# Starting a feed-forward network's activations 0 to 48 bytes into their buffers

## The chip, the cores and the metric

The kernel runs on one core of one Trainium2 chip. The time is the device time of one execution in microseconds (us); lower is better. TensorE multiplies matrices, ScalarE (ACT) and VectorE (DVE) do the element-wise work, and the on-chip memory that they share is SBUF: 128 partitions, each a long row of bytes. An operand of an instruction is a stretch of bytes at the same place in every partition. This document is about where in the partition such a stretch begins.

## The reference

The reference is a two-layer encoder over 256 tokens of width 2048, all in float32. Each layer has an attention half and a feed-forward half. Cut to what matters here, the feed-forward half is:

```
h = rmsnorm(x, norm_ffn[l]) * (1.0 + sc_m) + sh_m          # (256, 2048)
g, v = split(h @ w_up[l])                                  # 2 x (256, 5632)
u = silu(conv3(g)) * conv3(v)                              # depthwise over the tokens
x = x + gt_m * (u @ w_down[l])                             # back to (256, 2048)
```

The product `u` is what the kernel calls an activation; w_down is applied to it.

## The kernel before

**Layout.** Features lie on the 128 partitions and tokens along the partition, so the 5632 hidden features are 44 chunks of 128. A float32 number is kept as a sum of two numbers of a shorter type (fp32r): a high part and what is left over, the low part. An activation of one chunk is therefore `[P, 2, S]`: 256 high values and then 256 low ones, 2,048 bytes in a row of each partition. `split` (L349) writes them, the high half with an ACT instruction (L350) and the low half with a DVE one (L351).

**Products.** `feature_run` (L230) multiplies. For each block of weights and each activation there is a *wide* matmul, whose moving operand is all 512 columns of the activation (high and low) against the weights' high part (L248 or L253), and a *narrow* one, whose moving operand is the 256 high columns against the weights' low part (L250). The two together are called a *pair* below. With `joint` set there are three narrow ones instead (L239, L240, L241). The moving operand is the one that streams through TensorE; the stationary one is a 128x128 block of weights in `hl` and is loaded by an LDWEIGHTS (PEld in the profile) ahead of its matmul.

**Order.** The weights are read in units of 1 MB through four buffers, split into high and low parts by ACT (L225) and DVE (L226) into four `hl` buffers, and used in the order in which they arrive. The feed-forward half goes through the 44 chunks in three groups of 15, 16 and 13 (`FF_GROUPS`, L37; the loop at L830). For each group the up-projections fill the activations of the group, and then the down-projection (`down`, L869) runs over the 16 output blocks, each of which needs every chunk of the group. So each activation is the moving operand of 16 pairs; in the last group the last output block is joint, which makes 15 pairs and three narrow matmuls for each chunk. The tile planner orders each engine's instructions by their dependencies; the stretches that this document speaks of have no other order written by hand.

**Buffers.** `place` (L147) gives out the stage buffers. There are seven, known by a tag, and every use of a tag gets the same bytes: y0, y1, y2 (4 x 1,024 bytes in each partition), a, b0, b1 (12 x 1,024) and o (16 x 1,024). In the compiled program they lie one behind the other in that order, from byte 163,296 of the partition to byte 228,832:

| buffer | first byte | modulo 64 | modulo 512 | held by turns |
|---|---|---|---|---|
| y0, y1, y2 | 163296, 167392, 171488 | 32 | 480 | outputs of attention A, gate B, activations |
| a | 175584 | 32 | 480 | q, k, v of A; outputs of attention B; activations |
| b0, b1 | 187872, 200160 | 32 | 480 | q, k, v of B; outputs of attention B (b0); activations |
| o | 212448 | 32 | 480 | gate A; activations |

Everything else that TensorE reads as fp32r has its own place: the four `hl` buffers begin at byte 70,688, and the buffer that holds the normed input `h` or the merged branches `merged` begins at 103,456. These are all 32 modulo 64 and 32 modulo 512. Blocks within a buffer are multiples of 512 bytes apart, so these remainders hold for every fp32r operand. The padded rows `cpad` of the convolution are an exception of another kind: they are 1,032 bytes long, and ACT and DVE read and write them 0, 4 and 8 bytes from their start (L347, L824, L826).

The activations of the groups go into these buffers (two rows of 1,024 bytes for each chunk): groups 0 and 2 use o for eight chunks and a for the next (six in group 0, five in group 2), and group 0 puts its last chunk in y0; group 1 uses b0 and b1 for six each and y1 and y2 for two each.

Of the kernel before, what the change touches and what calls it, by code (L numbers as in the profile page):

```python
# [10 lines left out]
F32R = mybir.dt.float32r  # L11
# [4 lines left out]
P = 128  # L16
L = 2
D = 2048
S = 256
# [41 lines left out]

ATT = [1.288, 0.4]
ATT_B = [0.21, 0.21]

ADA_ORDER = [[p * KC + k for k in range(KC) for p in ps] for ps in ((0, 1), (2,), (3, 4), (5,))]
ADA_ORDER = [i for part in ADA_ORDER for i in part]
# [38 lines left out]
def encoder(ctx: ExitStack, tc: tile.TileContext, a: dict, out: bass.AP):  # L105
# [20 lines left out]
    for i in range(3):  # L126
        t = const.tile([P, S + 2], F32, name=f"cpad{i}")
# [16 lines left out]
    x = const.tile([P, KC, S], F32, name="x")  # L144
    sp = pool("s", 1)

    def place(tag, n, dt, name):  # L147
        return sp.tile([P, n, S], dt, name=name, tag=tag)

    mods, amods, nrms, done = {}, {}, {}, {0: 0, 1: 0}  # L150

# [197 lines left out]
    def split(dst, src):  # L349
        nc.scalar.copy(dst[:, 0], src)  # L350
        nc.vector.tensor_tensor(out=dst[:, 1], in0=src, in1=dst[:, 0].bitcast(F32), op=ALU.subtract)  # L351
# [169 lines left out]
    def urgent(yes):  # L521
        return tc.high_priority() if yes else nullcontext()
# [21 lines left out]
    def need(l, n):  # L544

        while done[l] < n:
            next(adas)
# [15 lines left out]

    mean_sq = sm.tile([P, 2], F32, name="ms_in", tag="nsa")
    acc = place("y0", 4, F32, "sq_in")
    for i in range(0, KC, 4):
        sq = acc if i == 0 else place(f"y{1 + i // 4 % 2}", 4, F32, f"sq_in{i}")
        nc.scalar.activation(out=sq[:], in_=x[:, i : i + 4], func=AF.Square)
        if i:
            nc.vector.tensor_tensor(out=acc[:], in0=acc[:], in1=sq[:], op=ALU.add)  # L570
# [31 lines left out]
    for l in range(L):  # L602
# [14 lines left out]


        packs = [place("a", 12, F32, f"packA{l}"), place("b0", 12, F32, f"packB{l}_0"), place("b1", 12, F32, f"packB{l}_1")]
        kTa, qTa = packs[0][:, 0:3:2], packs[0][:, 4:12]  # L620

# [125 lines left out]
        for mo in range(KC):  # L747
# [4 lines left out]
            st.features(oA, [proj_a], joint=joint)  # L752
        bg.pace(job, ATT_B[l])
        gb = []
        for tag in ("y0", "y1", "y2"):
            t = place(tag, 4, F32, f"gb{l}_{tag}")
            gb += [t[:, i] for i in range(4)]
        for i in range(2):
            t = ev.tile([P, 2, S], F32, name=f"gb{l}_{i}", tag="u", bufs=2)
# [22 lines left out]
        def residual(ps, mo, part, joint):  # L782

            gt = mod[:, part * KC + mo : part * KC + mo + 1]
            for half in ([slice(0, S)] if joint else [slice(S, 2 * S), slice(0, S)]):
                nc.vector.scalar_tensor_tensor(  # L786
                    out=x[:, mo], in0=ps[:, half], scalar=gt, in1=x[:, mo], op0=ALU.mult, op1=ALU.add
                )
# [30 lines left out]
        def conv(ps, ch, u):  # L819
            pad = cpad[ncp[0] % 3]  # L820
            ncp[0] += 1
            sum_halves(ps, pad[:, 1 : S + 1])
            w = cw[:, ch]
            nc.scalar.activation(out=u, in_=pad[:, 1 : S + 1], func=AF.Identity, scale=w[:, 1:2], bias=w[:, 3:4])  # L824
            for j, o in ((0, 0), (2, 2)):
                nc.vector.scalar_tensor_tensor(  # L826
                    out=u, in0=pad[:, o : o + S], scalar=w[:, j : j + 1], in1=u, op0=ALU.mult, op1=ALU.add
                )

        for gi, chunks in enumerate(FF_GROUPS):  # L830
            acts = []
            for tag, n in (("b0", 12), ("b1", 12), ("y1", 4), ("y2", 4)) if gi % 2 else (("o", 16), ("a", 12), ("y0", 4)):
                if len(acts) < len(chunks):
                    t = place(tag, n, F32R, f"act{l}_{gi}_{tag}")
                    acts += [t[:, i : i + 2] for i in range(0, n, 2)]
            acts = dict(zip(chunks, acts))
            sil = {}

            def g_evac(ps, c):
                u = sil[c] = ev.tile([P, 2, S], F32, name="u", tag="u", bufs=2)  # L840
                conv(ps, c, u[:, 0])
                nc.scalar.activation(out=u[:, 0], in_=u[:, 0], func=AF.Silu)

            def v_evac(ps, c):
                u = sil.pop(c)
                conv(ps, FC + c, u[:, 1])
                nc.vector.tensor_tensor(out=u[:, 1], in0=u[:, 1], in1=u[:, 0], op=ALU.mult)
                split(acts[c], u[:, 1])

            todo = list(chunks)  # L850
            if gi == 0:
                c0, c1 = todo[:2]
                todo = todo[2:]
                st.features(
                    hs, [lambda p: g_evac(p, c0), lambda p: v_evac(p, c0), lambda p: g_evac(p, c1), lambda p: v_evac(p, c1)]
                )
            for c in todo:
                st.features(hs, [lambda p: g_evac(p, c)])
                st.features(hs, [lambda p: v_evac(p, c)])
            if gi == len(FF_GROUPS) - 1:  # L860
                sums = Squares(f"ssf{l}") if l < L - 1 else None
            else:
                sums = None
            if gi == 0:
                need(l, 96)

            last = gi == len(FF_GROUPS) - 1

            def down(mo):  # L869
                def evac(ps):  # L870
                    residual(ps, mo, 5, last and mo >= ENDING)
                    if last:
                        if l < L - 1:
                            sums.add(mo)
                        else:
                            nc.sync.dma_start(out[:, mo], x[:, mo])

                return evac

            for mos in OUT_TURNS:  # L880
                end = mos[0] == KC - 1
                ending = last and mos[0] >= ENDING
                if last and end and l < L - 1:
                    nxt = Stream(l + 1)
                    nxt.prefetch(AHEAD)
                with urgent(ending):
                    st.features(
                        [acts[c] for c in chunks], [down(mo) for mo in mos], sums.first if sums and end else None, joint=ending
                    )
# [75 lines left out]
```

## Time and profile before

| | |
|---|---|
| median of 3 runs | 2775.12 us (2775.0 to 2776.88) |
| the profiled execution: its time | 2775.14 us |
| the profiled execution: its span, first to last instruction | 2773.4 us |
| mean granted TensorE clock | 0.991 |
| PE busy | 2715.0 us, 98% of the span |
| DVE busy, ACT busy | 2214.0 us (80%), 1450.3 us (52%) |

The profile is of one execution. An entry "L250 PE MATMUL ps<-act_o,hl" is a matmul issued at line 250, written to a tile named ps, with moving operand act_o (an activation in buffer o) and weights in hl. A matmul's own duration is longer than its turn, since the next one enters while it drains; the turn is the distance from one start to the next, and is read from views that merge a run of equal matmuls into one piece, or from a stretch's length over its matmuls. The chain of waits follows the work that ended last back from the end of the program.

### The profile page before, as it was taken

The page shows a single profiled execution, that of the slowest core. Times are in us where ns is not written, and L with a number is a line of the kernel's source. Part 1 is how long each engine was busy: PE and PEld are TensorE (multiplying, and loading weights), DVE is VectorE, ACT ScalarE, POOL GpSimd, SP SyncE. Part 2 cuts the span into 40 slices and gives each one's busy share as a digit, 9 for nine tenths or more (in the row PEclk, how much of TensorE's full clock was granted, in tenths as well). Part 3 has the DMA queues.
Part 4 walks back from the last instruction along what each step waited for, and adds up shares of the span by engine and source line. Part 5 has one row for each costly group of instructions (what it writes and reads, how often), then busy time and mean ns, then how long its engine had stood idle before and what let it go on. Part 6 is the DMA issues. An engine that isn't in the chain of part 4 may idle for free.

```text
span 2773.4 us, 39861 instructions
## 1 busy us (share of the span) xinstructions
PE 2715.0 (98%) x15930; PEld 2398.7 (86%) x15930; DVE 2214.0 (80%) x3163; ACT 1450.3 (52%) x2137; POOL 39.3 (1%) x24
## 2 busy tenths in 40 slices
PE   7899999999999999999999999999989999999999
PEld 5788799998888888888878888888878888888888
DVE  6998987897999888789976666768989767766775
ACT  5344684444654455355544567555455535544553
POOL 0000100000000000000000000000000000000000
PEclk9999999999999999999999999999999999999999
DMA  8887588896778766777756666665867655555553
GB/s 314 334 329 264 214 308 329 329 331 231 279 279 328 276 255 245 271 274 286 291 190 238 228 227 233 232 254 199 306 222 287 243 190 187 193 186 194 184 196 137
DMA packets 101852, 699.72 MB, mean 252 GB/s; under 512 B 12705, under 2 KB 15009, under 8 KB 17697
## 3 DMA queue, kind: packets, MB, share of 16 engines
q1 hardware_dynamic: 101666, 697.17, 68.2%
q8 instruction: 125, 2.05, 0.3%
q14 instruction: 61, 0.50, 0.1%
HBM read 695.03 MB, written 2.10 MB: 251 GB/s over the span
## 4 chain that ended last, share of the span: by engine, by line
PE 79%; issue 14%; DVE 4%; POOL 1%; ACT 1%; DMA 0%; POOLq 0%; SPq 0%; ACTq 0%; DVEq 0%
PE ps L253 20%; PE ps L250 18%; PE ps L248 15%; PE ps_t L338 4%; PE ps L240 4%; PE ps L239 4%; PE ps L241 4%; PE ps_t L339 4%; PE ps_t L337 4%; DVE aw L162 1%; DVE hl L226 1%; POOL qrs L390 1%; PE sc L485 1%; PE po L516 1%; ACT hl L225 0%
## 5 line engine op out<-in xcount | busy, mean ns | idle before, releaser
L226 DVE TENSOR_TENSOR hl<-w,hl 128x1024 fp32r<-128x1024 f32 x928 | 1131.3, 1223 | 307.6 <-ACT hl L225 300.8
L225 ACT CAST hl<-w 128x1024 fp32r<-128x1024 f32 x928 | 972.5, 1050 | 756.3 <-PE ps L253 174.5
L162 DVE CUSTOM_DVE_ANT_0 aw<-aw,cact,ab 128x2048 f32<-128x2048 f32 x192 | 450.7, 2347 | 25.5 <-DMA aw<-in_aw 25.1
L250 PEld LDWEIGHTS ps<-h,hl 128*128 128x128 f32 x3328 | 428.0, 191 | 16.9
L250 PE MATMUL ps<-h,hl 128*128 128x256 f32 x3328 | 432.9, 283 | 0.0
L253 PE MATMUL ps<-h,hl 128*128 128x512 f32 x1712 | 428.7, 392 | 0.0
L248 PE MATMUL ps<-h,hl 128*128 128x512 f32 x1616 | 406.4, 394 | 5.5 <-DVE cpad L347 4.5
L248 PEld LDWEIGHTS ps<-h,hl 128*128 128x128 f32 x1616 | 306.3, 190 | 70.8 <-DVE cpad L347 5.4
L253 PEld LDWEIGHTS ps<-h,hl 128*128 128x128 f32 x1712 | 307.9, 189 | 55.0
L346 ACT COPY r<-ps 128x256 f32<-128x256 f32 x240 | 88.9, 372 | 286.0 <-PE ps L253 286.0
L337 PE MATMUL ps_t<-hl,h 128*128 128x512 f32 x576 | 228.1, 401 | 7.5 <-ACT hl L225 7.0
L338 PE MATMUL ps_t<-hl,h 128*128 128x512 f32 x576 | 228.6, 397 | 4.7 <-DVE hl L226 4.7
L339 PE MATMUL ps_t<-hl,h 128*128 128x512 f32 x576 | 227.6, 396 | 0.9 <-DVE h L426 0.9
L826 DVE SCALAR_TENSOR_TENSOR u<-cpad,cw,u 128x256 f32<-128x256 f32 x352 | 168.7, 481 | 7.6 <-ACT u L824 3.2
L241 PE MATMUL ps<-h,hl 128*128 128x256 f32 x512 | 145.9, 285 | 0.0
L239 PE MATMUL ps<-h,hl 128*128 128x256 f32 x512 | 145.3, 284 | 0.0
L240 PE MATMUL ps<-h,hl 128*128 128x256 f32 x512 | 145.0, 283 | 0.0
L786 DVE SCALAR_TENSOR_TENSOR x<-ps,mod,x 128x256 f32<-128x256 f32 x237 | 111.5, 481 | 40.5 <-PE ps L253 30.4
L337 PEld LDWEIGHTS ps_t<-hl,h 128*128 128x128 f32 x576 | 109.8, 191 | 31.1 <-ACT hl L225 7.6
L338 PEld LDWEIGHTS ps_t<-hl,h 128*128 128x128 f32 x576 | 110.0, 191 | 30.8 <-DVE hl L226 8.1
L339 PEld LDWEIGHTS ps_t<-hl,h 128*128 128x128 f32 x576 | 109.9, 191 | 24.3 <-DVE h L426 1.4
L347 DVE TENSOR_TENSOR cpad<-ps,r 128x256 f32<-128x256 f32 x176 | 74.4, 424 | 63.2 <-ACT r L346 63.0
(202 smaller groups left out, 3610.4 us busy)
## 6 DMA issues: line engine op xcount, KB each, us to landing
w<-in_ws SPq DMA_DIRECT2D x464, 1024.0 KB, 4.9
aw<-in_aw SPq DMA_DIRECT2D x192, 1024.0 KB, 4.9
bias<-in_bias SPq DMA_DIRECT2D x16, 256.0 KB, 4.4
x<-in_xT SPq DMA_DIRECT2D x4, 512.0 KB, 5.6
out<-x SPq DMA_DIRECT2D x16, 128.0 KB, 1.8
cw<-in_cw SPq DMA_DIRECT2D x2, 176.0 KB, 4.0
maskA<-in_maskA SPq DMA_DIRECT2D x1, 256.0 KB, 5.3
ab<-in_ab SPq DMA_DIRECT2D x2, 48.0 KB, 7.1
```

What stands on the lines that cost most here:

```text
L162: nc.vector.tensor_tensor_reduce(out=raw[:], in0=raw[:], in1=cact[:], scale=1.0, scalar=ab[:, i : i + 1], op0=ALU.mult, op1=ALU.add, accum ...
L225: nc.scalar.copy(hl[:, 0], r)
L226: nc.vector.tensor_tensor(out=hl[:, 1], in0=r, in1=hl[:, 0].bitcast(F32), op=ALU.subtract)
L239: nc.tensor.matmul(out[:, 0], hi, act[:, 0], start=first, stop=False)
L240: nc.tensor.matmul(out[:, 0], hi, act[:, 1], start=False, stop=False)
L241: nc.tensor.matmul(out[:, 0], lo, act[:, 0], start=False, stop=last)
L248: nc.tensor.matmul(o, w, act, start=first, stop=False)
L250: nc.tensor.matmul(o, w, act, start=False, stop=False)
L253: nc.tensor.matmul(o, w, act, start=False, stop=last)
L337: nc.tensor.matmul(ps[:], xh, hi, start=kc == kcs[0], stop=False)
L338: nc.tensor.matmul(ps[:], xh, lo, start=False, stop=False)
L339: nc.tensor.matmul(ps[:], xl, hi, start=False, stop=kc == kcs[-1])
```

## The change

`place` makes each stage buffer 16 elements (64 bytes) longer and takes an optional `skip` in bytes, by which the view that it returns is moved into the buffer. Seven buffers 64 bytes longer lie one behind the other, so each also moves by 64 bytes for each buffer ahead of it, whatever it holds. The activations alone ask for a skip, from a table by layer and group:

```
+ACT_SKIP = [
+    [{"o": 16, "a": 16}, {"b0": 16, "b1": 32}, {"o": 32, "a": 32}],
+    [{"o": 48, "a": 48}, {"b0": 32, "b1": 48}, {"o": 0, "a": 0}],
+]
...
-    def place(tag, n, dt, name):
-        return sp.tile([P, n, S], dt, name=name, tag=tag)
+    def place(tag, n, dt, name, skip=0):
+
+        t = sp.tile([P, n * S + 16], dt, name=name, tag=tag)
+        return t[:, skip // 4 : skip // 4 + n * S].rearrange("p (n s) -> p n s", s=S)
...
-                    t = place(tag, n, F32R, f"act{l}_{gi}_{tag}")
+                    t = place(tag, n, F32R, f"act{l}_{gi}_{tag}", ACT_SKIP[l][gi].get(tag, 0))
```

No instruction is added or removed, and none has another shape. Tags that are not in the table (y0, y1, y2) get no skip. What is computed stays the same.

## The prediction

> **What bounds the kernel now.** I read the page first, then the stages in which the activations are used, then the pace of single matmuls.
>
> ```profile
> span 2773.4 us, 39861 instructions
> PE 2715.0 (98%) x15930; PEld 2398.7 (86%) x15930; DVE 2214.0 (80%) x3163; ACT 1450.3 (52%) x2137; POOL 39.3 (1%) x24
> ...
> PE 79%; issue 14%; DVE 4%; POOL 1%; ACT 1%; DMA 0%; POOLq 0%; SPq 0%; ACTq 0%; DVEq 0%
> ```
>
> TensorE is busy for 98% of the span and carries the chain of waits. What an operand's place can change is therefore first of all the turn of a matmul. The activations are read in the six down-projections (layer 0 groups 0, 1, 2, then layer 1). One row for each, from the view of stretches:
>
> ```profile
> core 0: us, PE busy (x) PEld busy (x) DVE busy (x) ACT busy (x) POOL busy (x), PEclk, DMA share, GB/s
> 843.50:926.90 83.40, 83.40 (x482) 72.63 (x482) 72.91 (x92) 32.69 (x33) 0.00 (x0) 1.00 0.83 319
> 1104.90:1193.80 88.90, 88.90 (x514) 77.40 (x513) 69.58 (x84) 34.87 (x35) 0.00 (x0) 1.00 0.70 262
> 1338.40:1411.00 72.60, 72.60 (x432) 63.53 (x430) 58.98 (x82) 33.47 (x44) 0.00 (x0) 1.00 0.70 256
> 2202.20:2285.60 83.40, 83.40 (x482) 72.66 (x481) 51.41 (x65) 32.75 (x33) 0.00 (x0) 1.00 0.54 190
> 2463.60:2552.50 88.90, 88.90 (x514) 77.40 (x513) 55.21 (x67) 34.86 (x35) 0.00 (x0) 1.00 0.54 192
> 2697.10:2769.40 72.30, 72.30 (x430) 63.27 (x428) 42.62 (x57) 25.38 (x26) 0.00 (x0) 1.00 0.43 152
> sum 489.50, PE 489.50 PEld 426.89 DVE 350.71 ACT 194.02 POOL 0.00; mean PE 81.58 PEld 71.15 DVE 58.45 ACT 32.34 POOL 0.00
> ```
>
> In all six, PE busy equals the length of the stretch at a granted clock of 1.00: nothing is waited for, and every nanosecond that a matmul gains or loses here moves the end by as much. The whole lever is 489.5 us. DVE is the next engine (72.91 of 83.40 us), so TensorE could be 10 us faster in that stage before DVE's splitting of weights limits it.
>
> Now the pace. The chain, first in an up-projection (moving operand h), then in the first down-projection (activations); columns are start, length, what:
>
> ```profile
> 806.55 1.91 PE ps L250 x16
> 808.47 1.84 PE ps L253 x8
> 810.31 1.81 PE ps L248 x8
> ...
> ```
> ```profile
> 845.57 1.83 PE ps L250 x16
> 847.40 1.86 PE ps L253 x8
> 849.26 0.91 PE ps L250 x8
> 850.17 1.86 PE ps L253 x8
> ```
>
> A narrow matmul takes 1.91/16 = 119.4 ns with h and 0.91/8 = 113.75 ns with an activation. A wide one takes 230 then 226.3 ns with h (1.84/8, 1.81/8; mean 228.1) and 232.5 ns with an activation (1.86/8). The sums are nearly equal: 347.5 ns for a pair with h, 346.25 ns with an activation. The same difference shows where all matmuls are narrow, layer 0's projection of the outputs of attention B (oB, 384 matmuls) and the output projection behind it (merged, 768 matmuls):
>
> ```profile
> 524.50:568.04 43.54, 43.54 (x386) 1.00 0.78 288
> 568.04:660.44 92.40, 92.40 (x772) 1.00 0.89 327
> ```
>
> 43.54/384 = 113.4 ns and 92.40/768 = 120.3 ns. Clock, form and code are the same; oB begins at 480 modulo 512 and merged at 32, like the weights. So the place of a moving operand relative to the weights seems to have a price, some 6.9 ns a matmul, and the wide ones pay it where the narrow ones don't. All fp32r operands of this trace begin 32 past a multiple of 64: what 16, 48 or 0 past such a multiple costs, no row shows.
>
> **The change part by part.** With 64 bytes more for each buffer the starts without skip become, modulo 512: y0 480, y1 32, y2 96, a 160, b0 224, b1 288, o 352; all are still 32 modulo 64. The skips are added to that, so it is a skip of 32 that reaches a multiple of 64, and not a skip of 0. Counted in pairs (16 for a chunk; 15 in the last groups, with three narrow ones beside):
>
> - 16 or 48 past a multiple of 64 (skips 16 and 48): 14 + 14 chunks of both groups 0, b0 of layer 0 and b1 of layer 1, 40 chunks, 640 pairs.
> - a multiple of 64 (skip 32): 13 chunks of layer 0's group 2 (195 pairs, 39 narrow), b1 of layer 0, b0 of layer 1 (192): 387 pairs.
> - still 32 past: 10 chunks in y0, y1, y2 and the 13 of layer 1's group 2: 355 pairs. With the others that is 1382; all but y0's 32 change place relative to the weights, 1350.
>
> *Writing.* ACT and DVE write the activations, 88 instructions each. Whether their place has a price is shown by cpad, which is written and read 4 bytes off, against aligned tiles:
>
> ```profile
> L347 DVE TENSOR_TENSOR cpad<-ps,r x176: 414/426/428, 696.6 to 2697.7; 128x256 f32<-128x256 f32 x176
> L347 DVE TENSOR_TENSOR z<-ps,r x48: 418/425/426, 1750.9 to 1930.2; 128x256 f32<-128x256 f32 x48
> ```
> ```profile
> L350 ACT CAST act_o<-u x32: 388/407/408, 702.2 to 2645.6; 128x256 fp32r<-128x256 f32 x32
> L351 DVE TENSOR_TENSOR act_o<-u,act_o x32: 417/418/423, 704.2 to 2646.6; 128x256 fp32r<-128x256 f32 x32
> ```
>
> 426 against 425 ns: nothing. I take 0. The cover would be the up-projections, in which the chain runs on TensorE; if writing took twice as long and that cover were gone it would be 88 x (407 + 418) = 73 us, and a gain is bounded by the same cover at 0.
>
> *Place relative to the weights, activations.* Bounds for a pair from the chain's rows: best 113.75 + 226.3 = 340.0 ns, worst 119.4 + 232.5 = 351.9, so -6.2 to +5.7 ns against 346.25, and for 1350 pairs -8.4 to +7.7 us. At both places that the trace shows the price falls on one of the two and the sum hardly differs, so I take the nearest known sum for each: the 64 pairs of y1 (at 32, as h) +1.25 ns, 0.1 us; 0 for the others.
>
> *The same for the attention's outputs, layer 0, three narrow matmuls for each head and output block.* oB: 384 matmuls, a at 160 and b0 at 224, between the known 480 (113.4) and 32 (120.3). Bounds 0 (no run of narrow ones is faster) and 384 x 6.9 = 2.6 us; neither end is nearer, I take half, 1.3 us. Attention A's outputs in y1 and y2 (two heads each, 96 matmuls each): y1 at 32 pays it all, 0.7 us; y2 half, 0.3 us. In layer 1 these are pairs: 0.
>
> *The start itself, 640 pairs at 16 or 48, 387 at 0.* Nothing in the trace prices it. Nearest rows: cpad (0) on the low side, and the 6.9 ns step on the high side, as what one more access might cost: 640 x 2 x 6.9 = +8.8 us for the first, and the same step as a gain, 387 x 2 x 6.9 + 39 x 6.9 = -5.6 us, for the second. I take 0 for both, by cpad, the only row where a start is off, though on another engine. [...]
>
> *The longer buffers* shift addresses and nothing else; no DMA, wait or instruction is added, and none is moved in a queue (SP's and POOL's included).
>
> Sum: 0.1 + 1.3 + 0.7 + 0.3 = +2.4 us on 2775.14 us of the profiled execution (span 2773.4 and 1.7 around it; the median of the runs, 2775.12, is the same): **2777.5 us**. A change under 0.2% (5.6 us) is about what a measurement of this kernel can't tell from none, so my forecast is "no change".
>
> **The rivals.**
>
> *Slower, one more access (2786 us).* If a start 16 past a multiple of 32 costs each read one more access of 6.9 ns: +8.8 us. For it speaks that TensorE's turn does depend on low address bits (113.4 against 120.3); against it, that the step seen belongs to the relation with the weights. Past 5.6 us with the +2.4 it decides from (5.6 - 2.4)/1280 = 2.5 ns a matmul.
>
> *Much slower, halved reading.* If TensorE fetches in aligned 32-byte words and a start of 16 splits each of them, 640 pairs take up to twice their turn: 640 x 346.25 = +222 us, 2999 us. Nothing in the trace speaks for it but that it never happens there: all starts are 32 past.
>
> *Faster (2769 us).* If the present start of 32 past a multiple of 64 already costs an access in every matmul, the 387 pairs gain 5.6 us, and another 387 x 6.2 = 2.4 us if their wide ones go at 226.3 ns: -8.0 us, 2769.5. For it: no start on a multiple of 64 has been seen, so the pace of now may not be TensorE's own. Against: narrow and wide differ by 226.3 - 113.75 = 112.5 ns for 256 columns, so most of a turn is proportional to the columns and no fixed extra shows. [...]
>
> **How the numbers follow.** No price of the start, place within ±5.6 us: 0.45, 2777.5 us. One more access: 0.24. Halved, wholly or in part: 0.12. Faster: 0.19. So faster 0.19, same 0.45, slower 0.24 + 0.12 = 0.36. The range leaves out the halved reading (0.12) and little else: up to 2777.5 + 8.8 + 7.7 + 1.3, about 2795 (one more access and the worst place together), down to 2769.5 with some 3.5 us of the gain by place, 2766.
>
> **What would show it.** The six stretches of the down-projections keep their lengths: 83.4, 88.9 and 72.6 us in layer 0. Layer 0's group 0 against layer 1's group 0 tells 16 from 48; group 2 of layer 0 against that of layer 1 tells 0 from 32 modulo 64. oB's 113.4 ns rise toward 120. One more access shows as both groups 0 longer by 14 x 16 x 13.8 ns = 3.1 us; halved reading as over 100 us there. L350 and L351 stay at 407 and 418 ns. The prediction is wrong if a moving operand's pace depends on 16 or 64 bytes, or if the planner, given buffers of another shape, orders the instructions differently.

## The result: 0.28% slower

The changed kernel takes 2781.68 us (median of 12 runs, 2779.99 to 2787.64) against 2774.22 us (12 runs, 2772.51 to 2776.88): ratio 1.0028, 95% interval 1.0019 to 1.0037. The profiled execution took 2779.99 us.

The page of the changed kernel:

```profile
span 2778.2 us, 39861 instructions
...
PE 2717.4 (98%) x15930; PEld 2402.4 (86%) x15930; DVE 2215.0 (80%) x3163; ACT 1449.4 (52%) x2137; POOL 39.3 (1%) x24
```

The same instructions, in the same order on every engine, and TensorE is still the bound. The stretches that matter, in the changed kernel: first layer 0's projection of oB, then the six down-projections (start and end, length, busy time of each engine, granted clock):

```profile
core 0: us, PE busy (x) PEld busy (x) DVE busy (x) ACT busy (x) POOL busy (x), PEclk, DMA share, GB/s
523.49:569.14 45.65, 45.65 (x387) 45.65 (x385) 43.92 (x72) 21.56 (x31) 0.00 (x0) 1.00 0.77 287
843.25:927.63 84.38, 84.38 (x482) 73.70 (x481) 73.04 (x92) 32.63 (x33) 0.00 (x0) 1.00 0.84 316
1105.62:1195.76 90.14, 90.14 (x514) 78.65 (x513) 69.72 (x84) 34.79 (x35) 0.00 (x0) 1.00 0.69 258
1340.37:1414.13 73.76, 73.76 (x432) 64.52 (x430) 58.95 (x82) 33.56 (x44) 0.00 (x0) 1.00 0.68 253
2204.83:2289.01 84.18, 84.18 (x482) 73.46 (x481) 51.36 (x65) 32.70 (x33) 0.00 (x0) 1.00 0.52 189
2467.00:2557.03 90.03, 90.03 (x514) 78.49 (x513) 55.20 (x67) 34.82 (x35) 0.00 (x0) 1.00 0.54 189
2701.63:2774.28 72.65, 72.65 (x430) 63.81 (x428) 42.60 (x57) 25.32 (x26) 0.00 (x0) 1.00 0.44 152
```

The down-projections sum to 495.1 us, 5.6 us more than before (489.5), each still wholly busy at a granted clock of 1.00. oB's projection takes 45.65 us instead of 43.54, 2.1 us more. Together 7.7 us, about the 7.5 us by which the medians differ. (The two profiled executions differ by only 4.9 us. The one of the changed kernel starts oB 1.0 us earlier, it is 1.4 us shorter between oB and the first down-projection, and 0.5 us shorter between the down-projections of layer 0 and those of layer 1. The opening part differs from kernel to kernel: oB starts at 522.6 to 525.7 us in the runs below that leave `h` where it was.)

The pace, from the changed kernel's chain in the first down-projection (start, length, what):

```profile
845.26 1.90 PE ps L257 x16
847.16 1.85 PE ps L260 x8
849.01 0.95 PE ps L257 x8
849.96 1.85 PE ps L260 x8
```

A narrow matmul (L257, formerly L250) now takes 0.95/8 = 118.75 ns instead of 113.75, a wide one 1.85/8 = 231 instead of 232.5. Further on the same chain has pieces of 0.93 and 1.87 us (116 and 234 ns); the pair takes 350 ns in either case, 3.75 ns more than before. Over the whole stretch, from each start to the next, the narrow ones go from 114.0 to 118.5 ns on average and the wide ones from 232.8 to 232.4, so the loss lies in the narrow ones. It isn't confined to what moved: buffer y0 is first in the pool and has no skip, so the chunk in it begins where it did. In the first down-projection its narrow matmuls last 277 ns each before and 282 after, with 113.9 and 118.1 ns from each start to the next (the groups of that stretch; behind the bar busy us, then mean ns), first before, then after:

```profile
L250 PE MATMUL ps<-act_y,hl 128*128 128x256 f32 x16 | 4.1, 277 | 0.0
```
```profile
L257 PE MATMUL ps<-act_y,hl 128*128 128x256 f32 x16 | 4.2, 282 | 0.0
```

### The profile page after: what moved, and what is told of

Read it like the earlier page. It is cut to its first block, busy times and chain, and to the rows that moved or that the text cites. A ratio compares the mean times of both kernels' runs of the same rounds, so it can differ in the third digit from the quotient of the medians.

```text
span 2778.2 us, 39861 instructions
## 1 busy us (share of the span) xinstructions
PE 2717.4 (98%) x15930; PEld 2402.4 (86%) x15930; DVE 2215.0 (80%) x3163; ACT 1449.4 (52%) x2137; POOL 39.3 (1%) x24
## 4 chain that ended last, share of the span: by engine, by line
PE 79%; issue 14%; DVE 4%; POOL 1%; ACT 1%; DMA 1%; POOLq 0%; SPq 0%; ACTq 0%; DVEq 0%
PE ps L260 19%; PE ps L257 18%; PE ps L255 15%; PE ps_t L345 4%; PE ps_t L346 4%; PE ps L246 4%; PE ps L247 4%; PE ps L248 4%; PE ps_t L344 4%; DVE aw L169 1%; DVE hl L233 1%; POOL qrs L397 1%; PE sc L492 1%; PE po L523 1%; DMA aw<-in_aw 0%
## 5 line engine op out<-in xcount | busy, mean ns | idle before, releaser
L257 PEld LDWEIGHTS ps<-h,hl 128*128 128x128 f32 x3328 | 427.7, 191 | 16.9
L257 PE MATMUL ps<-h,hl 128*128 128x256 f32 x3328 | 432.7, 283 | 0.0
```

What stands on the lines that cost most here:

```text
L257: nc.tensor.matmul(o, w, act, start=False, stop=False)
```

## The experiments

Two theories to begin with. S: the start of an operand modulo 32 or 64 has a price. P: its place relative to the weights has one. *Distance* below is the start of the moving operand less that of the weights.

**The longer buffers alone.**

```
 ACT_SKIP = [
-    [{"o": 16, "a": 16}, {"b0": 16, "b1": 32}, {"o": 32, "a": 32}],
-    [{"o": 48, "a": 48}, {"b0": 32, "b1": 48}, {"o": 0, "a": 0}],
+    [{"o": 0, "a": 0}, {"b0": 0, "b1": 0}, {"o": 0, "a": 0}],
+    [{"o": 0, "a": 0}, {"b0": 0, "b1": 0}, {"o": 0, "a": 0}],
```

> The changed kernel with every skip set to 0: the buffers stay 64 bytes longer, so each moves by 64 bytes for each buffer ahead of it, and every start is again 32 past a multiple of 64. Theory P (what counts is where a moving operand lies relative to the weights in some stretch of up to 512 bytes): the loss stays; the six down-projections are together 4 to 7 us longer than before (489.5 us), the projection of oB in layer 0 takes about 45.6 us as in the changed kernel instead of 43.5, and the whole is about 0.25% slower than before. Theory S (what counts is the start modulo 32 or 64): the down-projections return to 83.4, 88.9, 72.6, 83.4, 88.9, 72.3 us and the whole is within 0.1% of before.

Ratio 1.0015 (1.0005 to 1.0025). The same stretches in this kernel:

```profile
522.57:568.21 45.64, 45.64 (x386) 45.64 (x385) 43.91 (x72) 21.58 (x31) 0.00 (x0) 1.00 0.79 287
843.84:927.67 83.83, 83.83 (x482) 73.47 (x481) 72.86 (x92) 32.57 (x33) 0.00 (x0) 1.00 0.85 319
1105.65:1195.10 89.45, 89.45 (x514) 78.17 (x513) 69.68 (x84) 34.85 (x35) 0.00 (x0) 1.00 0.71 261
1339.67:1412.51 72.84, 72.84 (x432) 64.02 (x430) 58.88 (x82) 33.53 (x44) 0.00 (x0) 1.00 0.68 256
2203.84:2287.67 83.83, 83.83 (x482) 73.47 (x481) 51.41 (x65) 32.65 (x33) 0.00 (x0) 1.00 0.53 190
2465.65:2555.09 89.44, 89.44 (x514) 78.16 (x513) 55.21 (x67) 34.80 (x35) 0.00 (x0) 1.00 0.53 190
2699.66:2772.31 72.65, 72.65 (x430) 63.82 (x428) 42.61 (x57) 25.32 (x26) 0.00 (x0) 1.00 0.44 151
```

Without any skip, oB's loss is there in full (45.64) and the down-projections sum to 492.0 us, +2.5. So the skips add the other 3.1 us, and layer 1's group 2, whose skip was 0, has the same 72.65 us in both. The down-projections lost less than the 4 to 7 us expected by P, and the whole 0.15% instead of 0.25%. Still, 4.6 of the 7.7 us come from the longer buffers alone, with which every start stays 32 past a multiple of 64: S alone can't be it.

**The skip alone, in buffer o.** o is last in the pool, so only its own length changes.

```
-        t = sp.tile([P, n * S + 16], dt, name=name, tag=tag)
+        t = sp.tile([P, n * S + (16 if tag == "o" else 0)], dt, name=name, tag=tag)
...
+    [{"o": 16}, {}, {"o": 32}],
+    [{"o": 48}, {}, {"o": 0}],
```

> Only buffer o, the last one, is longer, and only the activations in it are skipped: 16, 32, 48 and 0 bytes in layer 0 groups 0 and 2 and layer 1 groups 0 and 2. Every other operand stays where it was before. o holds 8 of 15 or 13 chunks. Theory S: layer 0 group 0 and layer 1 group 0 become longer by the share of o, about 0.5 us each (8/15 of the 0.8 to 1.0 us lost in the changed kernel), and layer 0 group 2 by about 0.7 us. Theory P in its strict form (only whole steps of 64 bytes count): layer 0 group 0 at 48 stays at 83.4 us, and the other two change as far as they pass into the next 64 bytes. The second groups and layer 1 group 2 stay at 88.9 and 72.3 us by both.

Ratio 1.0013 (1.0004 to 1.0022). The three groups with a skip:

```profile
843.30:927.82 84.52, 84.52 (x482) 73.64 (x481) 73.07 (x92) 32.64 (x33) 0.00 (x0) 1.00 0.84 315
...
1339.32:1412.72 73.40, 73.40 (x432) 64.35 (x430) 58.88 (x82) 33.54 (x44) 0.00 (x0) 1.00 0.71 254
2202.55:2287.00 84.45, 84.45 (x482) 73.61 (x481) 51.44 (x65) 32.71 (x33) 0.00 (x0) 1.00 0.53 188
```

+1.1, +0.8 and +1.05 us; the other three groups kept their lengths to 0.1 us. Steps of 16 bytes count, which the strict form of P had not allowed. The cost in both groups 0 is twice the 0.5 us that S gave for o's share (in layer 0's group 2 it is near S's 0.7): a little over half of the activations moved, and layer 0's group 0 lost more than in the changed kernel (84.38), where nearly all had moved.

**Everything moved by 32 bytes, and the stage buffers moved together.** In the first kernel the distances stay and all starts become multiples of 64; in the others the stage buffers move as one block, by X bytes (64, 128, 32 and 256), and the weights, `h` and `merged` stay.

```
-    mean = const.tile([P, 1], F32, name="mean")
+    mean = const.tile([P, 9], F32, name="mean")[:, :1]
```
```
-    one = sm.tile([1, P], F32, name="one", tag="one", bufs=1)
+    one = sm.tile([1, P + X // 4], F32, name="one", tag="one", bufs=1)
```

> The kernel before with everything behind the first constants moved by 32 bytes: weights, h, merged and all stage buffers now begin at a multiple of 64, and their distances from each other are as before. Theory P (the distance to the weights counts): every stage keeps its length to 0.1 us, oB's projection 43.5 us, the down-projections 83.4, 88.9, 72.6 us. Theory S (the start modulo 64 counts): the turn of nearly every matmul changes; by one access of 6.9 ns saved in each, the 15,000 matmuls would give back some 100 us.

> The kernel before with all seven stage buffers moved together by 64 bytes, so that they begin at 32 modulo 512 like the weights, and like h and merged. Theory P: the projection of oB in layer 0 takes 384 x 120.3 = 46.2 us instead of 43.5, and a narrow matmul on activations takes 119 to 120 ns and a wide one about 228, so that the down-projections change by less than 0.5 us each. Theory S: no stage changes, since every start stays 32 past a multiple of 64; oB 43.5 us.

> As before with all stage buffers moved together by 128 bytes, to 96 modulo 512. Theory P with a period of 128 bytes: nothing changes, oB 43.5 us and 83.4, 88.9, 72.6 us. Theory P with a longer period: oB between 43.5 and 46.2 us, and the down-projections differ from both the kernel before and the one moved by 64. Theory S: nothing changes.

> Only the stage buffers moved together, by 32 bytes: they begin at a multiple of 64 (0 modulo 512) and the weights stay at 32. Theory P: the narrow matmuls go as in the skipped buffer o of the run before that stood at 0, about 118 ns instead of 113.8, the wide ones about 232.5; the down-projections of groups 0 become 0.5 to 1.2 us longer and oB's projection of layer 0 goes to about 45.3 us. Theory S: a multiple of 64 is not slower than 32 past one.

> The stage buffers moved together by 256 bytes, to 224 modulo 512. If the pattern repeats every 256 bytes, every stage is as in the kernel before: oB 43.5 us, groups 0 at 83.4 us. If its period is 512 or longer, oB is between 43.5 and 46.2 us and the groups 0 differ by some tenths of a us.

Each of these five was run once: 2772.4 us with everything moved by 32, and 2784.0, 2780.8, 2775.9 and 2776.1 us with the stage buffers moved by 32, 64, 128 and 256. The medians of the kernel before beside them were 2773.9 and 2775.2 us, so what follows rests on the stretches. Two of each, oB's projection and layer 0's group 0. Everything by 32:

```profile
523.29:566.83 43.54, 43.54 (x387) 43.54 (x386) 41.79 (x69) 22.15 (x31) 0.00 (x0) 1.00 0.80 290
841.07:924.44 83.37, 83.37 (x482) 72.63 (x481) 72.87 (x92) 32.67 (x33) 0.00 (x0) 1.00 0.83 318
```

The stage buffers by 32:

```profile
523.84:569.28 45.44, 45.44 (x387) 45.44 (x385) 42.34 (x69) 22.00 (x31) 0.00 (x0) 1.00 0.78 279
844.79:929.33 84.54, 84.54 (x482) 73.72 (x481) 73.09 (x92) 32.63 (x33) 0.00 (x0) 1.00 0.84 315
```

By 64:

```profile
525.65:571.73 46.08, 46.08 (x386) 46.08 (x385) 44.00 (x72) 21.59 (x32) 0.00 (x0) 1.00 0.79 284
847.22:931.14 83.92, 83.92 (x482) 73.97 (x481) 72.88 (x92) 32.70 (x33) 0.00 (x0) 1.00 0.85 319
```

By 128:

```profile
524.90:570.13 45.23, 45.23 (x387) 45.23 (x385) 43.56 (x71) 21.53 (x31) 0.00 (x0) 1.00 0.81 291
845.67:928.66 82.99, 82.99 (x482) 72.98 (x481) 72.86 (x92) 32.64 (x33) 0.00 (x0) 1.00 0.86 320
```

By 256:

```profile
524.61:568.15 43.54, 43.54 (x387) 43.54 (x385) 41.78 (x69) 22.13 (x31) 0.00 (x0) 1.00 0.79 287
843.80:927.17 83.37, 83.37 (x482) 72.64 (x481) 72.79 (x92) 32.77 (x33) 0.00 (x0) 1.00 0.84 320
```

This settles S for multiples of 32: with every start on a multiple of 64 and the distances unchanged, both stretches are as before to 0.03 us, where S gave some 100 us over the whole kernel; on the same multiples of 64 with another distance they are 1.9 and 1.1 us longer. What counts here is where the moving operand lies relative to what did not move with it. That this partner is the weights is argued: they are the only other operand of these matmuls, but `h`, the buffers of the raw weights and most other tiles ahead of the stage buffers kept their places with them, and no run moved the weights alone. Moved by 256 bytes, both stretches are as before (43.54 and 83.37 us), while 128 bytes change them (45.23 and 82.99 us): as far as these places show, the pattern repeats every 256 bytes. A start 16 past a multiple of 32 with an unchanged distance wasn't tried; there S stays open as an addition.

**Moving h and merged too.** h and merged stand at the weights' own place, distance 0. Here they get a distance of 448 (192 modulo 256, as the stage buffers have it), of 64, and of 128 (`H_SKIP`). The buffer grows by as much, and `one` is 64 bytes longer as above, so that all stage buffers lie at the same distance modulo 256.

```
+    def wide_h(name):
+        t = hp.tile([P, H_SKIP // 4 + KC * 2 * S], F32R, name=name, tag="h")
+        return t[:, H_SKIP // 4 :].rearrange("p (k i s) -> p k i s", k=KC, i=2)
...
-        h = hp.tile([P, KC, 2, S], F32R, name=f"h{l}_{w}", tag="h")
+        h = wide_h(f"h{l}_{w}")
...
-        merged = hp.tile([P, KC, 2, S], F32R, name=f"merged{l}", tag="h")
+        merged = wide_h(f"merged{l}")
```

> The kernel before with h and merged moved to 480 modulo 512 as well (the stage buffers stay at 480, the weights at 32). Theory P: where all matmuls are narrow in layer 0 (both gates, 1536 matmuls of h, and the output projection, 768 of merged) the turn falls from 120.3 to 113.4 ns, -10.6 and -5.3 us; the up-projections (3328 pairs of h and 240 of merged) go from 347.5 to 346.3 ns a pair, some -4 us; together about 20 us or 0.7% faster than before. Theory S: no change, since all starts stay 32 past a multiple of 64.

> Weights at 32, and h, merged and all stage buffers at 96 modulo 512, 64 bytes ahead of them. With the stage buffers alone at 96 a pair took 345.3 ns (345.0 in the down-projections' length) against 347.5 to 349 for h at 32 and 346.3 at 224 or 480. If the place alone decides, the up-projections of both layers become 1 to 2 ns a pair shorter than with h at 480, each about 5 us shorter than before (495 us), the down-projections 0.2 to 0.4 us shorter than before, and the narrow stretches of layer 0 go at 117.8 ns (gates -5 us in all): 12 to 18 us faster than before, about 0.55%. If the rhythm that a stretch inherits from the one before it decides as much, the up-projections gain no more than the 2 us each that h at 480 gave.

> The same with h, merged and the stage buffers at 160 modulo 512, the one place in steps of 64 modulo 256 that no run has shown with all operands together. By the changed kernel, where the outputs of attention B stood at 160 among others, narrow matmuls take about 119 ns and wide ones 232: the up-projections would be 2 to 4 us longer than before and the whole within 0.3% of before. If a place alone has a steady turn, its intervals are as regular as at 32, 96 and 224.

The kernel before, layer 0's first up-projections and layer 1's gates:

```profile
671.14:843.54 172.40, 170.14 (x960) 149.62 (x961) 159.49 (x233) 102.57 (x161) 0.00 (x0) 0.98 0.73 267
1641.68:1885.20 243.52, 243.52 (x1398) 214.50 (x1396) 165.59 (x238) 149.33 (x244) 1.64 (x1) 1.00 0.63 234
```

h at 480, ratio 0.9958 (0.9946 to 0.9970): oB, the narrow matmuls of merged, then those two:

```profile
522.31:567.54 45.23, 45.23 (x387) 45.23 (x385) 43.56 (x71) 21.54 (x31) 0.00 (x0) 1.00 0.79 287
567.54:658.38 90.84, 90.84 (x772) 90.64 (x770) 76.62 (x93) 38.98 (x48) 0.00 (x0) 1.00 0.87 327
668.96:840.33 171.37, 169.08 (x960) 146.65 (x961) 159.29 (x233) 102.52 (x161) 0.00 (x0) 0.99 0.75 268
1637.37:1879.75 242.38, 242.38 (x1397) 211.22 (x1396) 165.42 (x238) 149.48 (x244) 1.64 (x1) 1.00 0.64 235
```

h at 96, ratio 0.9969 (0.9957 to 0.9981):

```profile
670.09:841.20 171.11, 168.84 (x960) 147.96 (x961) 159.39 (x233) 102.76 (x161) 0.00 (x0) 0.98 0.74 268
1639.21:1880.65 241.44, 241.44 (x1398) 212.38 (x1397) 165.27 (x238) 149.39 (x244) 1.64 (x1) 1.00 0.65 236
```

h at 160, a single run, 2804.2 us against 2775.0:

```profile
677.27:851.75 174.48, 172.25 (x961) 149.81 (x962) 159.96 (x233) 102.64 (x161) 0.00 (x0) 0.98 0.72 264
1660.15:1905.39 245.24, 245.24 (x1398) 214.36 (x1397) 165.78 (x238) 149.48 (x244) 1.64 (x1) 1.00 0.64 233
```

The direction was right and the sizes weren't. With h at 480 the gain is 0.42%, not 0.7%: oB stands where it did, relative to the same weights, and yet takes 45.23 us instead of 43.54 (117.8 ns a matmul instead of 113.4); merged goes at 90.84/768 = 118.3 and not at 113.4. One place, two turns. The down-projections show none of this: layer 0's group 0 takes 83.37 us with h at 480 too. With h at 96 the six up-projections together gain 9.3 us, about the 10 expected, but the whole gains 0.31% instead of 0.55%. Part of that goes back where the roles are exchanged, in the q, k, v projections: there the weights stream and h is loaded. Their 1728 matmuls last 2 to 3 ns longer each, and where they follow one another without a break the median from start to start is 233 ns instead of 227 (one of the three groups, before and at 96):

```profile
L338 PE MATMUL ps_t<-hl,h 128*128 128x512 f32 x576 | 228.6, 397 | 4.7 <-DVE hl L226 4.7
```
```profile
L344 PE MATMUL ps_t<-hl,h 128*128 128x512 f32 x576 | 230.1, 400 | 4.5 <-DVE hl L232 4.5
```

At 160 both stretches shown are slower than before, by 2.1 and 1.7 us, and the expected "within 0.3%" was wrong by far: 1.05% slower in that one run.

**Is the turn inherited?** Only merged moves; h stays at 32. All buffers are as in the kernel with h at 480, so that for oB only h's place differs between the two. Against the kernel before:

```
+H_SKIP = 448
...
+    def wide_h(name, skip=0):
+        t = hp.tile([P, H_SKIP // 4 + KC * 2 * S], F32R, name=name, tag="h")
+        return t[:, skip // 4 : skip // 4 + KC * 2 * S].rearrange("p (k i s) -> p k i s", k=KC, i=2)
...
-        h = hp.tile([P, KC, 2, S], F32R, name=f"h{l}_{w}", tag="h")
+        h = wide_h(f"h{l}_{w}")
...
-        merged = hp.tile([P, KC, 2, S], F32R, name=f"merged{l}", tag="h")
+        merged = wide_h(f"merged{l}", H_SKIP)
```

> Only merged moves to 480 modulo 512; h stays at 32, the stage buffers at 480 and the weights at 32, as in the kernel before. In layer 0 the stretch of oB (narrow matmuls) then follows on h at 32, as in the kernel before, and merged follows on oB. If a stretch of narrow matmuls keeps the rhythm in which it begins, oB takes 43.5 us (113.4 ns) and merged goes on at 113.4 ns: its 768 matmuls become 5.3 us shorter than the 92.4 us of before. If the place alone decides, oB and merged go as with h at 480: oB 45.2 us and merged at 117.9 ns, 1.7 us shorter than before. The whole is 0.1 to 0.3% faster than before.

Ratio 0.9982 (0.9972 to 0.9992). oB, then the narrow matmuls of merged:

```profile
525.63:569.17 43.54, 43.54 (x387) 43.54 (x385) 41.78 (x69) 22.15 (x31) 0.00 (x0) 1.00 0.80 290
569.17:656.96 87.79, 87.79 (x772) 87.41 (x770) 77.30 (x96) 38.77 (x49) 0.00 (x0) 1.00 0.92 340
```

oB is back at 43.54 us, and merged at the same 480 now takes 87.79 us where it took 90.84 with h at 480 too: 4.6 us less than before, close to the 5.3 expected. At one distance oB has two turns, 113.4 and 117.8 ns, and merged 114.3 and 118.3. Which of the two comes depends on the stretch ahead: for oB that is a stretch of h, which no matmul of oB reads and which alone had moved; merged follows oB's turn both times. How a turn is handed on, no run shows.

## Why the prediction was partly right

The range (2766 to 2795) held the time, and slower had 0.36. That isn't owed to the access of 8.8 us in its upper end, which was not paid: the bounds by place alone (7.7 us for the activations, 2.6 for oB) reach past 2785 us. The forecast itself, "no change" at 2777.5, fell short: 2781.7 is 0.28% slower, and the interval (0.19 to 0.37%) tells it from none.

- *Which part carries it.* Right: all the loss that can be placed lies in the matmuls' turns, and none in writing, where the changed kernel's L357 and L358 still take 407 and 418 ns as L350 and L351 did. The planner kept its order.
- *The start itself, 0.* Right for 32 against 0 modulo 64 (everything by 32: 83.37 us against 83.40). "One more access" gave 3.1 us in both groups 0; they lost 1.0 and 0.8, and the group on a multiple of 64 lost 1.2, which that rival would have left alone. "Halved reading" and "faster by a multiple of 64" are refuted by the same stretches. Whether a start at 16 or 48 has a small price of its own stays open, since those operands also changed their distance.
- *Place relative to the weights, activations: 0.1 us.* This is the step that failed. "At both places that the trace shows the price falls on one of the two and the sum hardly differs, so I take the nearest known sum": the sum at two places was taken for the sum at all. Measured: +5.6 us for the down-projections, inside the bounds of -8.4 to +7.7; 2.5 of it comes with the longer buffers alone, and 3.1 with the skips, which for 16 and 48 bytes don't tell place from start. Moved together, a group of 240 pairs takes, at a distance of 192 modulo 256, 83.37 us, at 0 83.92, at 64 82.99 and at 224 84.54: the two known places (192 and 0) lie between a better and a worse one.
- *oB in layer 0: 1.3 us, half of the bounds.* 2.1 us; layer 1's oB, taken as 0, became 0.6 us longer (44.4 to 44.9 us). Attention A's share (1.0 us) can't be read from its stretch, which is interleaved with the attention and differs between kernels that leave it alone. Its last 105 matmuls in a row take 12.62 us instead of 12.29, 3.1 ns more each; at that rate, an estimate, the 384 of layer 0 lose 1.2 us. With these the placed loss is some 9.5 us rather than 7.7, within the interval of the medians (5.3 to 10.3 us).
- *A price of a place.* The working gave each operand a price by its own place. The narrow matmuls of the chunk in y0, which didn't move, last 5 ns longer too (282 against 277), and oB at one place has two turns (113.4 and 117.8 ns). In both the price isn't the operand's own: it goes with the matmuls around it, and where all matmuls are narrow with the stretch ahead.
- *A slip.* The table of buffers names y1 and y2 the wrong way round (y2 lies ahead of y1), so y2 moved to 32 and y1 to 96. Both hold two heads of attention A and two chunks of each group 1, and the sum is the same.

## What to carry to other kernels

When matrix products with a weight load before each bound a kernel, as here, look first at where the moving operand lies relative to the stationary one: here oB took 45.23 to 46.08 us with the stage buffers moved by 32, 64 or 128 bytes, and its old 43.54 us with them moved by 256 or with everything moved by 32. Lengthening a buffer by 64 bytes moves all that lie behind it; pad to a multiple of 256 bytes, or choose the distance on purpose: moving h and merged by 448 bytes made this kernel 0.42% faster than before. Measure the stretch in its own surroundings, since the stretch ahead can set its turn too, as with oB (113.4 or 117.8 ns) and merged (114.3 or 118.3).

## What the runs showed of the hardware that was not expected

- At one granted clock (1.00) the turn of an fp32r matmul of 256 columns (oB, 384 of them) is 113.4 ns with the stage buffers where they were or 256 bytes on, and 118.3, 120.0 and 117.8 ns with them moved by 32, 64 and 128 bytes; with everything moved by 32 together it stays at 113.4. Steps of 16 bytes count too: with 8 of 15 chunks moved by 16, a down-projection took 84.5 us instead of 83.4.
- One distance has two turns (43.54 and 45.23 us for the 384 matmuls of oB at the same place), and which of them comes depends on the place of the operand streamed in the stretch ahead (h at 32 or at 480). Why the distance and the stretch ahead have a price, no run shows.
